# First norm rearranged with tables loaded later on; experts' output biases and the list of further rounds made behind the tenth expert

## The chip, the cores and the metric

One Trainium2 chip; the program runs on one of its cores. The metric is the device time of one execution in microseconds (us), as the median of several runs.

## What is computed

A decoder layer on 256 tokens of width 1024, all in float32: a norm whose scale and shift come from a condition vector, a mixer (softmax attention and gated linear attention side by side), a second norm and a mixture of 32 experts of which each token uses four, a final norm. Cut to what the change touches:

```
c_act = jax.nn.silu(c)
mod = (c_act @ w_ada[l] + b_ada[l])[:, None, :]
shift1, scale1, gate1, shift2, scale2, gate2 = jnp.split(mod, 6, axis=-1)
h = _rmsnorm(x, norm1_w[l]) * (1.0 + scale1) + shift1
x = x + gate1 * _mixer(h, w_in[l], gla_gate_w[l], gla_gate_b[l], gla_norm_w[l], w_o_moba[l], w_o_gla[l], b_merge[l], w_out[l])   # h @ w_in first, 1024 x 9232
h = _rmsnorm(x, norm2_w[l]) * (1.0 + scale2) + shift2
x = x + gate2 * _moe(h, w_router[l], b_router[l], w_exp_in[l], b_exp_in[l], w_exp_out[l], b_exp_out[l])
return _rmsnorm(x, final_norm_w)

# inside _moe, for the rows of expert e
hid = tokens[rows] @ w_exp_in[e] + b_exp_in[e]   # 1024 -> 2048
out = _clamped_swiglu(hid) @ w_exp_out[e] + b_exp_out[e]
out = out * wts[:, None]
```

One expert's weights are 8 MB (in) and 4 MB (out); the 32 of them are 403 MB of the 480 MB that the kernel moves.

## The kernel before

**Start.** The four quarters of x come transposed (`x0[u]`, 128 features by two by 256 tokens). Their squares are taken, two quarters on VectorE and two on ScalarE (`sx`). TensorE sums them over the features with 16 small products against a column of ones (into `pn_`), ScalarE takes the root (`rs1`), VectorE the reciprocal, TensorE spreads it over the partitions, ScalarE copies that to `rst`, and `scaled_x` multiplies x by it. Scale and shift of the norm are rows `cact @ w_ada`: `ada_rows(j)` makes those of features 256j to 256j+255 with eight products, from two blocks of `w_ada` of 1 MB each (`la[j][0]`, `la[j][1]`), and copies them out; `norm_unit` turns the rows into columns (`turn_rows`), adds the bias (`modT`, `s1`) and makes the normed features `hf`, their rounded half `hh` and the rest `hl`.

**First product.** It runs over j (four pairs of 128 features) and n (six blocks of 256 columns of w_in): `quarter` is 12 matmuls. Each weight block is split first into a rounded half `wh` (a copy on ScalarE, `split_hi`) and the rest `wl` (a subtraction on VectorE, `split_lo`); `splits(PAHEAD)` runs four blocks ahead. The weights come through a ring of 80 KB per partition (`ring`) in an order that is written out (`la`, `lw`); the first 80 KB are asked for at once, all on SyncE's queue (SP), later ones as blocks are used up (`Load.used`). The small weights `wgl` (16 columns of w_in) and `gw` come on ScalarE's queue.

**Mixer.** Everything up to the experts is written in an order that a planner makes as the program is built; the change does not move anything between the first product and the end of the mixer, except that the biases `b_exp_in` (`braw`) are asked for there.

**Experts.** The loop over e makes the hidden layer of expert e (`hidden`: 64 matmuls over four weight tiles), then the output of expert e - 1 (`output`: 32 matmuls over two tiles). For every second expert the rows of the next pair are gathered, and the finished pair is added into the four output banks `y` (`scatter`, called from within the next hidden layer through `later` and `between`). A tile is 2 MB; nine tiles fit, in rotation, so SP asks for a tile as soon as the tile nine places before it has been used up by TensorE:

```
rings = [ring] * 4 + [phase["r"]] * (RING2 // WE) + [ring]
def next_ring():
    rings.append(rings.pop(0))
    return rings[-1]
```

Around this loop stand two pieces of work that belong to no expert. `accumulators`, after the first hidden layer, turns the weights of the tokens (`wT`), spreads the second gate (`g2`) and multiplies the output biases `bo` by it; the function that it returns, called after the output of expert 0, adds the biases to `y` with four matmuls. `further_rounds`, after the output of expert 1, lists the experts that have more tokens than one round takes; the list is read only after the loop.

## Time and profile before

| | |
|---|---|
| median of 3 runs | 1297.88 us (1296.58 to 1302.86) |
| profiled execution, its own time | 1301.64 us |
| its span, first to last instruction | 1299.8 us |
| TensorE busy | 1227.0 us, 94% |
| VectorE, ScalarE, GpSimd busy | 422.1 us (32%), 294.2 us (23%), 7.6 us (1%) |
| moved | 480.13 MB, mean 369 GB/s |

A busy TensorE is not TensorE at its peak: matmuls are pipelined, and a slower clock shows as busy time too. The share of busy time is a mean over stages; what a change is worth in a stage is read from that stage. The first product starts at 22.6 us, the experts at 372.5 us. In the timeline "x8" counts what one line did in a stretch, and a float32 matmul counts as two.

### The profile page before, as it was taken

The page shows a single profiled execution, that of the slowest core. Times are in us where ns is not written, and L with a number is a line of the kernel's source. Part 1 is how long each engine was busy: PE and PEld are TensorE (multiplying, and loading weights), DVE is VectorE, ACT ScalarE, POOL GpSimd, SP SyncE. Part 2 cuts the span into 40 slices and gives each one's busy share as a digit, 9 for nine tenths or more (in the row PEclk, how much of TensorE's full clock was granted, in tenths as well). Part 3 has the DMA queues.
Part 4 walks back from the last instruction along what each step waited for, and adds up shares of the span by engine and source line. Part 5 has one row for each costly group of instructions (what it writes and reads, how often), then busy time and mean ns, then how long its engine had stood idle before and what let it go on. Part 6 is the DMA issues. An engine that isn't in the chain of part 4 may idle for free. (4 is left out here: it accounts for less than half of the span.)

```text
span 1299.8 us, 16460 instructions
## 1 busy us (share of the span) xinstructions
PE 1227.0 (94%) x6844; PEld 667.0 (51%) x6844; DVE 422.1 (32%) x849; ACT 294.2 (23%) x614; POOL 7.6 (1%) x13
## 2 busy tenths in 40 slices
PE   7999999999999899999999989898989989898995
PEld 5899989989854343443434424243433324242432
DVE  2567588866532211121112211111112212111112
ACT  2466567654321010110101101010101101010102
POOL 0000000000010000000000000000000000000000
PEclk9999999999899899999999999999999999999999
DMA  8997589584979999999999999999999999999994
GB/s 267 336 328 222 203 165 225 197 323 163 347 292 426 375 397 430 429 431 430 430 431 430 428 431 430 430 430 430 431 430 432 428 429 431 430 430 430 431 430 189
DMA packets 73436, 480.13 MB, mean 369 GB/s; under 512 B 7472, under 2 KB 24000, under 8 KB 48784
## 3 DMA queue, kind: packets, MB, share of 16 engines
q1 hardware_dynamic: 69664, 476.07, 92.0%
q10 hardware_dynamic: 3552, 2.69, 0.6%
q8 instruction: 55, 0.90, 0.3%
q0 software_dynamic: 144, 0.30, 0.1%
q14 instruction: 21, 0.17, 0.0%
HBM read 477.99 MB, written 1.05 MB: 369 GB/s over the span
## 5 line engine op out<-in xcount | busy, mean ns | idle before, releaser
L1306 PE MATMUL h<-w,xg 128*64 128x512 f32 x2048 | 464.4, 600 | 15.6 <-DMA w<-in_w_exp_in_dram 15.5
L1306 PEld LDWEIGHTS h<-w,xg 128*64 128x64 f32 x2048 | 140.6, 137 | 298.4 <-issue 269.4
L1340 PE MATMUL g<-w,aT 128*64 128x512 f32 x1024 | 232.3, 603 | 28.0 <-DMA w<-in_w_exp_out_dram 24.0
L1319 DVE TENSOR_SCALAR sg<-h 128x512 f32<-128x512 f32 x32 | 22.1, 692 | 520.0 <-PE h L1306 510.0
L400 PE MATMUL ps_a<-m,wh 128*128 128x256 f32 x896 | 172.0, 293 | 3.7 <-ACT m L510 3.7
L1340 PEld LDWEIGHTS g<-w,aT 128*64 128x64 f32 x1024 | 73.5, 138 | 172.9 <-issue 149.0
L400 PEld LDWEIGHTS ps_a<-m,wh 128*128 128x128 f32 x896 | 144.0, 197 | 6.8 <-ACT m L510 3.8
L1332 ACT COPY aT<-g 128x512 f32<-128x512 f32 x32 | 18.7, 586 | 506.2 <-PE g L1330 506.2
L400 PE MATMUL ps_a<-m,wl 128*128 128x256 f32 x448 | 129.1, 288 | 0.6 <-DVE wl L386 0.6
L386 DVE TENSOR_TENSOR wl<-w,wh 128x512 fp32r<-128x512 f32 x176 | 115.6, 685 | 38.7 <-ACT wh L382 37.3
L382 ACT CAST wh<-w 128x512 fp32r<-128x512 f32 x176 | 105.0, 617 | 67.2 <-PE ps_a L400 50.8
L1346 DVE TENSOR_TENSOR u<-g,u 64x512 f32<-64x512 f32 x64 | 44.1, 689 | 195.2 <-PE g L1340 194.5
L400 PEld LDWEIGHTS ps_a<-m,wl 128*128 128x128 f32 x448 | 88.2, 197 | 0.8 <-DVE wl L386 0.8
L1320 ACT ACTIVATE sg<-sg 128x512 f32<-128x512 f32 x32 | 20.2, 631 | 187.3 <-DVE sg L1319 187.3
L1239 PE MATMUL g<-Psel,u 128*128 128x128 f32 x512 | 60.4, 276 | 0.0
L1352 PE MATMUL y<-u,pT 128*128 128x512 f32 x128 | 59.2, 605 | 0.8 <-DVE u L1346 0.8
L1239 PEld LDWEIGHTS g<-Psel,u 128*128 128x128 f32 x512 | 58.5, 192 | 0.1
L1248 ACT ACTIVATE xg<-xg,shift 128x128 f32<-128x128 f32 x128 | 40.9, 390 | 27.7 <-DVE xg L1245 26.2
L1352 PEld LDWEIGHTS y<-u,pT 128*128 128x128 f32 x128 | 23.0, 189 | 36.8 <-issue 34.7
L400 PE MATMUL ps_a<-u,wh 128*128 128x256 f32 x224 | 40.7, 283 | 0.0
L400 PE MATMUL ps_a<-wh,m 128*128 128x256 f32 x192 | 34.9, 284 | 0.0
L400 PEld LDWEIGHTS ps_a<-u,wh 128*128 128x128 f32 x224 | 34.4, 189 | 0.0
(301 smaller groups left out, 887.0 us busy)
## 6 DMA issues: line engine op xcount, KB each, us to landing
w<-in_w_exp_in_dram SPq DMA_DIRECT2D x128, 2048.0 KB, 37.3
w<-in_w_exp_out_dram SPq DMA_DIRECT2D x63, 2048.0 KB, 37.7
w<-in_w_in_dram SPq DMA_DIRECT2D x26, 1024.0 KB, 14.3
w<-in_w_ada_dram SPq DMA_DIRECT2D x16, 1024.0 KB, 9.6
w<-in_w_ada_dram SPq DMA_DIRECT2D x32, 256.0 KB, 6.9
w<-in_w_in_dram SPq DMA_DIRECT2D x12, 512.0 KB, 8.0
w<-in_w_o_gla_dram SPq DMA_DIRECT2D x4, 1024.0 KB, 8.6
w<-in_w_o_moba_dram SPq DMA_DIRECT2D x4, 1024.0 KB, 7.1
```

Of the source, the lines that this page charges most:

```text
L382: S.copy(wh, wv)
L386: V.tensor_tensor(wl, wv, wh.bitcast(F32), op=OP.subtract)
L400: PE.matmul(o, lhsT, rhs, start=(b + k + n == 0), stop=(k == 7 and n == 2), skip_group_check=True)
L1239: PE.matmul(o, flat(hx[t, q])[:, 128 * kk:128 * kk + 128], P[:, t], start=(n == 0), stop=(n == 3))
L1248: S.activation(xg[:, kk, 0:w_], xg[:, kk, 0:w_], AF.Identity, bias=shift2[:, kk:kk + 1])
L1306: PE.matmul(ph[64 * hf_:64 * hf_ + 64, 512 * b:512 * b + 512], xg[:, k, SL * i:SL * i + SL], wi[k // 2][:, k % 2, 1024 * hf_ + 512 * b:102 ...
L1319: V.tensor_scalar(sg_, ph[:, 0::2], LIMIT, None, op0=OP.min)
L1320: S.activation(sg_, sg_, AF.Sigmoid, scale=ALPHA)
L1332: S.copy(aT, ps.rearrange("p (c s) -> p c s", c=4))
L1340: PE.matmul(po[64 * n:64 * n + 64, :], aT[:, cc, 64 * hf_:64 * hf_ + 64], wo[hf_][:, cc, 512 * n:512 * n + 512], start=(hf_ + cc == 0), st ...
L1346: V.tensor_mul(flat(og[n])[64 * par:64 * par + 64], po[64 * n:64 * n + 64], flat(g2[n])[64 * n:64 * n + 64])
L1352: PE.matmul(y[t, n], pT[0:rows, 128 * t:128 * t + 128], flat(og[n])[0:rows], start=False, stop=True, skip_group_check=True)
```

## The change

Six edits, in the order of the program.

1. `wgl` is laid out on the host, so that each partition reads one run of 512 bytes in place of eight of 64 bytes.
2. The blocks of `w_ada` come as two transfers in place of four, and the first blocks of `w_in` as one in place of two, with runs of 4 KB in place of 2 KB. Bytes, order and ring stay as they were.
3. The table for the root is asked for at once behind the sigmoid (`scrap`). VectorE adds the squares up, so that TensorE sums them with 2 products in place of 16. `ada_rows` is cut into halves: the first runs ahead of the sum of squares, the second behind the spreading of the reciprocal; the copy `rst` comes ahead of the copy of the rows.
4. `norm_unit(0)` comes ahead of `splits(PAHEAD)`.
5. `braw` is asked for on GpSimd's queue; `bo` is a tile of its own with one transfer.
6. `accumulators` is cut in two: `second_gate` stays, `add_biases` comes after the output of expert 12, its four matmuls within the hidden layer of expert 14; `further_rounds` comes after the output of expert 9.

```diff
-    return {"vec": np.ascontiguousarray(vec.T), "xf": np.ascontiguousarray(xf)}
+    thin = lambda w: np.ascontiguousarray(w.reshape(8, 128, -1).transpose(1, 0, 2).reshape(128, -1))
+    return {"vec": np.ascontiguousarray(vec.T), "xf": np.ascontiguousarray(xf),
+            "wgl": thin(np.asarray(inputs["w_in"])[0][:, C_GL:C_GL + 16])}
...
-                for k in range(0, 4, 2):
-                    for v in range(2):
-                        nc.sync.dma_start(wa[:, k:k + 2, v], kview(w_ada, D * v + 256 * j, D * v + 256 * j + 256,
-                                                                   4 * i + k, 4 * i + k + 2))
+                for v in range(2):
+                    nc.sync.dma_start(wa[:, :, v], kview(w_ada, D * v + 256 * j, D * v + 256 * j + 256,
+                                                         4 * i, 4 * i + 4))
...
-        def first_block(j, n0, n1):
+        def first_block(j, c0, c1):
             def emit():
-                wa = ring.tile([128, n1 - n0, 2, 512], F32, name="w")
-                for n in range(n0, n1):
-                    nc.sync.dma_start(wa[:, n - n0],
-                                      kview(w_in, C_GQ + 512 * n, C_GQ + 512 * n + 512, 2 * j, 2 * j + 2))
+                wa = ring.tile([128, 2, c1 - c0], F32, name="w")
+                nc.sync.dma_start(wa, kview(w_in, C_GQ + c0, C_GQ + c1, 2 * j, 2 * j + 2))
                 return wa
-            return queue(emit, 2 * (n1 - n0), 4 * KB * (n1 - n0))
+            return queue(emit, (c1 - c0) // 256, 8 * (c1 - c0))
...
+        scrap = mwork.tile([128, 1], F32, name="scrap")
         S.activation(cact, vec[:, R_C:R_C + 8], AF.Sigmoid)
+        S.activation(scrap, epst, AF.Sqrt)
         sx = [unit() for _ in range(4)]
-        for u in range(2):
-            V.tensor_mul(sx[2 * u], x0[2 * u], x0[2 * u])
-            S.activation(sx[2 * u + 1], x0[2 * u + 1], AF.Square)
-            if u == 0:
-                V.tensor_mul(cact, cact, vec[:, R_C:R_C + 8])
+        V.tensor_mul(sx[0], x0[0], x0[0])
+        S.activation(sx[1], x0[1], AF.Square)
+        V.tensor_mul(cact, cact, vec[:, R_C:R_C + 8])
+        V.tensor_mul(sx[2], x0[2], x0[2])
+        S.activation(sx[3], x0[3], AF.Square)
+        for u in (2, 1, 3):
+            V.tensor_tensor(sx[0], sx[0], sx[u], op=OP.add)
+        V.tensor_tensor(sx[0][:, 0], sx[0][:, 0], sx[0][:, 1], op=OP.add)
...
-        def ada_rows(j):
-
-            bk = Bank()
-            for i in range(2):
-                for k in range(4):
-                    PE.matmul(bk.t[32 * k:32 * k + 32, :], cact[:, 4 * i + k:4 * i + k + 1].to_broadcast([128, 32]),
-                              la[j][i].tv[:, k].rearrange("p v n -> p (v n)"), start=(i == 0), stop=(i == 1),
-                              skip_group_check=True)
-                la[j][i].used()
-            ev = unit()[:, :, 0:T].rearrange("p a b -> p (a b)")
+        def ada_rows(j, bk, i):
+
+            for k in range(4):
+                PE.matmul(bk.t[32 * k:32 * k + 32, :], cact[:, 4 * i + k:4 * i + k + 1].to_broadcast([128, 32]),
+                          la[j][i].tv[:, k].rearrange("p v n -> p (v n)"), start=(i == 0), stop=(i == 1),
+                          skip_group_check=True)
+            la[j][i].used()
+
+        def rows_out(bk):
+            ev = unit().rearrange("p a b -> p (a b)")
             S.copy(ev, bk.t)
             return bk, ev
-        pn_ = Bank()
-        for u in range(4):
-            for b in range(2):
-                for t in range(2):
-                    PE.matmul(pn_.t[:, t:t + 1], sx[u][:, b, 128 * t:128 * t + 128], ones[:, 0:1],
-                              start=(u + b + t == 0), stop=(u + b == 4), skip_group_check=True)
+        pn_, pr_ = Bank(), Bank()
+        ada_rows(0, pr_, 0)
+        for t in range(2):
+            PE.matmul(pn_.t[:, t:t + 1], sx[0][:, 0, 128 * t:128 * t + 128], ones[:, 0:1], start=True, stop=True)
         S.activation(rs1, pn_.t[:, 0:2], AF.Sqrt, bias=epst, scale=1.0 / D)
-        rows0 = ada_rows(0)
         V.reciprocal(rs1, rs1)
         for t in range(2):
             PE.matmul(pn_.t[:, 128 + 128 * t:256 + 128 * t], rs1[:, t:t + 1].to_broadcast([128, 128]), ident,
-                      start=True, stop=True, skip_group_check=True)
+                      start=True, stop=True)
+        ada_rows(0, pr_, 1)
         rst = unit()[:, 0]
         S.copy(rst, pn_.t[:, 128:384])
         pn_.free()
+        rows0 = rows_out(pr_)
...
-        S.dma_start(flat(wgl)[:, 0:128].rearrange("p (k n) -> p k n", k=8), kview(w_in, C_GL, C_GL + 16, 0, 8))
+        S.dma_start(flat(wgl)[:, 0:128], a["wgl"])
...
+        mod_unit(0, rows0)
+        norm_unit(0)
         splits(PAHEAD)
-        norm_unit(0, rows0)
...
-                    nc.sync.dma_start(flat(braw[n])[32 * i:32 * i + 32, :], a["b_exp_in"][0][:, c0:c0 + 512])
+                    G.dma_start(flat(braw[n])[32 * i:32 * i + 32, :], a["b_exp_in"][0][:, c0:c0 + 512])
...
-    bo = []
-    for n in range(2):
-        bo.append(flat(unit())[0:NE])
-        G.dma_start(bo[n], a["b_exp_out"][0][:, 512 * n:512 * n + 512])
+    bo_ = moe.tile([NE, 2, 512], F32, name="bo")
+    G.dma_start(bo_.rearrange("e n c -> e (n c)"), a["b_exp_out"][0])
+    bo = [bo_[:, n] for n in range(2)]
...
-    def accumulators():
-
-        wT = ew.tile([NE, T], F32, name="wT", bufs=1)
-        tp = psg.tile([128, 512], F32, name="g")
-        for t in range(2):
-            PE.transpose(tp[0:NE, 128 * t:128 * t + 128], wts[:, t], ident)
-        V.tensor_copy(wT, tp[0:NE, 0:T])
+    def second_gate():
+
         for n in range(2):
             ps = psg.tile([128, 512], F32, name="g")
             spread(ps, modT[:, 5, 4 * n:4 * n + 4])
             g2.append(unit())
             S.copy(flat(g2[n]), ps)
+
+    def add_biases():
+
+        wT = ew.tile([NE, T], F32, name="wT", bufs=1)
+        tp = psg.tile([128, 512], F32, name="g")
+        for t in range(2):
+            PE.transpose(tp[0:NE, 128 * t:128 * t + 128], wts[:, t], ident)
+        S.copy(wT, tp[0:NE, 0:T])
+        for n in range(2):
             V.tensor_mul(bo[n], bo[n], flat(g2[n])[0:NE])
...
-            add_biases = accumulators()
+            second_gate()
...
-        if e == 1:
-            add_biases()
-        if e == 2:
+        if e == 10:
             further_rounds()
+        if e == 13:
+            later.append(add_biases())
```

On TensorE the program begins so before: sums of squares (`ps_b<-ones,u`), rows (`y<-w,cact`), spreading (`ps_b<-kt,rs`), turning the rows (`y<-rows,u`), then the first product (`ps_a<-m,wh`).

```order
L365 MATMUL ps_b<-ones,u 128x1 x16
L353 MATMUL y<-w,cact 32x512 x8
L371 MATMUL ps_b<-kt,rs_182 128x128 x2
L345 MATMUL y<-rows,u 128x1 x4
L400 MATMUL ps_a<-m,wh 128x256 x2
```

And so in the change:

```order
L355 MATMUL y<-w,cact 32x512 x4
L368 MATMUL ps_b<-ones,u 128x1 x2
L372 MATMUL ps_b<-kt,rs_173 128x128 x2
L355 MATMUL y<-w,cact 32x512 x4
L349 MATMUL y<-rows,u 128x1 x4
L403 MATMUL ps_a<-m,wh 128x256 x2
```

Fourteen small matmuls are gone, and half of the rows stand ahead of the sum.

On ScalarE, at the same place, before: the root (`rs<-ps_b`), the copies of the rows and of `rst`, the two small transfers, four copies `wh`, then `hh` (`m<-u,modT,s`).

```order
L367 ACT_TABLE_LOAD
L367 ACTIVATE rs_182<-ps_b,epst 128x2
L358 COPY u<-y 128x512
L374 COPY u<-ps_b 128x256
L583 DMA u<-in_w_in_dram 128x8x16
L584 DMA u<-in_gla_gate_w_dram 16x512
L382 CAST wh<-w 128x512 x4
L510 ACTIVATE m<-u,modT,s_181 128x256 x2
```

In the change:

```order
L332 ACT_TABLE_LOAD
L332 ACTIVATE scrap<-epst 128x1
L335 ACTIVATE u<-u 128x512
L338 ACTIVATE u<-u 128x512
L369 ACTIVATE rs_173<-ps_b,epst 128x2
L376 COPY u<-ps_b 128x256
L362 COPY u<-y 128x512
L588 DMA u<-in_wgl_dram 128x128
L589 DMA u<-in_gla_gate_w_dram 16x512
L515 ACTIVATE m<-u,modT,s_172 128x256 x2
L385 CAST wh<-w 128x512 x6
```

The copies `wh` have moved behind `hh`, and VectorE's `wl` behind `hl` in the same way.

On TensorE behind the output of expert 0 (`g<-w,aT`), before: the way back of the next pair, the biases (`y<-u,wT`), the hidden layer of expert 2 (`h<-`), the output of expert 1 and the list (`g<-msk,ones`, `g<-kt,itc`).

```order
L1340 MATMUL g<-w,aT 64x512 x16
L1258 MATMUL g<-kt,pw 128x128 x2
L1215 MATMUL y<-u,wT 128x512 x4
L1298 MATMUL h<-bx,sel 128x512 x2
L1306 MATMUL h<-w,xg 64x512 x20
L1330 MATMUL g<-kt,li 128x128 x4
L1306 MATMUL h<-w,xg 64x512 x12
L1340 MATMUL g<-w,aT 64x512 x16
L1365 MATMUL g<-msk,ones 128x32 x2
L1376 MATMUL g<-kt,itc 1x128 x2
L1298 MATMUL h<-bx,sel 128x512 x2
```

In the change the same stretch reads:

```order
L1351 MATMUL g<-w,aT 64x512 x16
L1269 MATMUL g<-kt,pw 128x128 x2
L1309 MATMUL h<-bx,sel 128x512 x2
L1317 MATMUL h<-w,xg 64x512 x20
L1341 MATMUL g<-kt,li 128x128 x4
L1317 MATMUL h<-w,xg 64x512 x12
L1351 MATMUL g<-w,aT 64x512 x16
L1309 MATMUL h<-bx,sel 128x512 x2
```

The four matmuls of the biases and the four of the list are gone from it; they stand behind the output of expert 9 (the list) and in the hidden layer of expert 14 (the biases).

## Rows read from the trace of the kernel before

**Rows 1.** What TensorE waited for from 0 to 372 us, longest first: us in total, times, longest.

```profile
PE ps_b L365 <- DVE u L334: 5.7, 1, 5.7
PE ps_a L400 <- ACT m L510: 3.7, 1, 3.7
PE ps_a L1145 <- DVE msk L1142: 1.3, 1, 1.3
```

**Rows 2.** Timeline of the start, 0 to 36 us: start, duration (both us), engine, line, operation, output and inputs, shapes, count, and in brackets the idle time before and what ended it. DVE is VectorE, ACT is ScalarE.

```profile
5.69 6.99 PE L365 MATMUL ps_b<-ones,u 128*128 128x1 f32 x32 [5.69 <-DVE u L334]
...
7.87 0.63 ACT L335 ACTIVATE u<-u 128x512 f32<-128x512 f32 x1 [0.93 <-DMA u<-in_xf_dram]
...
8.52 1.28 ACT L367 ACT_TABLE_LOAD   x1
...
12.61 3.64 PE L353 MATMUL y<-w,cact 128*32 128x512 f32 x16
12.71 0.26 ACT L367 ACTIVATE rs<-ps_b,epst 128x2 f32<-128x2 f32 x1 [2.92 <-PE ps_b L365]
13.01 0.17 DVE L369 RECIPROCAL rs<-rs 128x2 f32<-128x2 f32 x1 [6.20 <-ACT rs L367]
...
16.18 1.22 PE L371 MATMUL ps_b<-kt,rs 128*128 128x128 f32 x4
16.31 0.58 ACT L358 COPY u<-y 128x512 f32<-128x512 f32 x1 [3.33 <-PE y L353]
...
17.19 1.71 PE L345 MATMUL y<-rows,u 128*128 128x1 f32 x8
...
17.84 0.69 DVE L580 TENSOR_TENSOR u<-u 128x512 f32<-128x512 f32 x1 [4.67 <-ACT u L374]
...
18.50 2.18 ACT L382 CAST wh<-w 128x512 fp32r<-128x512 f32 x4 [0.69 <-DMA w<-in_w_ada_dram]
...
21.56 0.15 DVE L498 TENSOR_TENSOR modT<-y,vec 128x4 f32<-128x4 f32 x1
...
21.95 1.09 ACT L510 ACTIVATE m<-u,modT,s 128x256 fp32r<-128x256 f32 x2 [1.27 <-DVE s L501]
...
22.60 1.05 PE L400 MATMUL ps_a<-m,wh 128*128 128x256 f32 x2 [3.71 <-ACT m L510]
```

**Rows 3.** Transfers of w_ada by the time at which SP issued them, KB each, median us from issue to landing: first the one issued from 3.1 us on (the fourth, last of block 0), then the one issued at 7.86 us (the eighth, last of block 1).

```profile
w<-in_w_ada_dram SPq DMA_DIRECT2D x1, 256.0 KB, 6.4
...
w<-in_w_ada_dram SPq DMA_DIRECT2D x1, 256.0 KB, 4.6
```

**Rows 4.** What SP's queue waited for from 0 to 40 us (`u<-in_w_in_dram` is the transfer of `wgl`, issued at 17.44 us), and the stretch from 20 to 22 us (stretch, its length, busy time of each engine with instructions, granted TensorE clock, share of the DMA engines, GB/s).

```profile
SPq L268 <- DMA u<-in_w_in_dram: 4.2, 1, 4.2
...
20.00:22.00 2.00, 0.00 (x0) 0.00 (x0) 1.93 (x6) 0.73 (x3) 0.00 (x0) 1.00 0.24 37
```

**Rows 5.** Timeline of the first product on TensorE, early and late in it; the third matmul of each three has a row of its own between these.

```profile
24.31 0.63 PE L400 MATMUL ps_a<-m,wh 128*128 128x256 f32 x2
...
24.95 0.63 PE L400 MATMUL ps_a<-m,wh 128*128 128x256 f32 x2
...
28.75 0.40 PE L400 MATMUL ps_a<-m,wh 128*128 128x256 f32 x2
...
29.11 0.40 PE L400 MATMUL ps_a<-m,wh 128*128 128x256 f32 x2
```

**Rows 6.** Stretches of the experts: stretch, its length, busy time and instructions of PE, PEld (weight loads), DVE, ACT and POOL, granted TensorE clock, share of the DMA engines, GB/s.

```profile
420.00:440.00 20.00, 20.00 (x74) 6.66 (x74) 0.00 (x0) 0.59 (x1) 0.57 (x1) 0.83 0.84 342
...
460.00:480.00 20.00, 20.00 (x108) 9.40 (x108) 4.49 (x10) 3.93 (x11) 0.00 (x0) 1.00 0.97 382
480.00:500.00 20.00, 20.00 (x96) 6.99 (x94) 2.07 (x4) 0.96 (x2) 0.00 (x0) 1.00 1.00 421
...
500.00:520.00 20.00, 20.00 (x84) 6.78 (x80) 4.34 (x9) 0.63 (x1) 0.00 (x0) 1.00 1.01 431
...
700.00:720.00 20.00, 18.34 (x84) 5.95 (x80) 3.84 (x6) 1.22 (x2) 0.00 (x0) 1.00 1.01 429
```

**Rows 7.** Timeline of TensorE in the first experts (columns as in rows 2): the hidden layer of expert 1, the biases, the hidden layer of expert 2, the first matmuls of the list, the hidden layer of expert 3.

```profile
392.24 8.80 PE L1306 MATMUL h<-w,xg 128*64 128x512 f32 x40
...
418.51 4.55 PE L1215 MATMUL y<-u,wT 32*128 32x512 f32 x8
...
424.15 10.72 PE L1306 MATMUL h<-w,xg 128*64 128x512 f32 x40
...
447.64 0.63 PE L1365 MATMUL g<-msk,ones 128*128 128x32 f32 x4
...
453.21 4.70 PE L1306 MATMUL h<-w,xg 128*64 128x512 f32 x16
```

**Rows 8.** Timeline of SP's queue: start, and the time from the first issue to the end of the last in the row. L138 issues the tiles of w_exp_in, L996 `braw`. The rows with x4 are the tiles of experts 3, 6 and 12.

```profile
324.48 9.99 SPq L996 DMA_DIRECT2D u<-in_b_exp_in_dram  x8
...
407.07 23.02 SPq L138 DMA_DIRECT2D w<-in_w_exp_in_dram  x4
...
499.59 11.44 SPq L138 DMA_DIRECT2D w<-in_w_exp_in_dram  x4
...
657.87 11.45 SPq L138 DMA_DIRECT2D w<-in_w_exp_in_dram  x4
```

**Rows 9.** Timeline of GpSimd from 360 us on: the first work on the biases `braw`.

```profile
369.86 0.61 POOL L1185 CAST bx<-u 128x512 fp32r<-128x512 f32 x1 [3.50 <-DVE wts L1161]
```

18 lines of the change are left out of this document (11 added, 7 removed).

## The prediction

> **What bounds the kernel now.** Three views were read in this order: the list of what TensorE waited for, the timeline of the start, and the stretches of the experts.
>
> Up to the experts TensorE sets the time. In the first 372 us it waits 5.7 us for the first squares, 3.7 us for `hh` ahead of the first product, and then never longer than 1.3 us at once [rows 1]. What the start gains, the whole mixer gains, as long as the weights keep up.
>
> In the experts the transfers set it. From 500 us on they run at 431 GB/s with the DMA engines full; TensorE is busy all of 500 to 520 us, but only 18.34 of the 20 us from 700 us on [rows 6], so by then it waits for weights. A tile of 2 MB takes 2.097 / 431 = 4.87 us, an expert (six tiles) 29.2 us. TensorE's own pace shows in SP's queue, which asks for a tile when TensorE has freed its place: from expert 6's tiles (499.59 us) to expert 12's (657.87 us) it took 158.3 us, 26.4 us for each [rows 8]. TensorE starts the experts behind the transfers, with all nine places full, and catches up 2.8 us per expert. While it is behind, a delay of TensorE frees a place late and the DMA engines idle; that time is never returned, since from then on they are full to the end. Such holes can be read: 342 GB/s from 420 to 440 us, 382 from 460 to 480 us, 421 from 480 to 500 us [rows 6].
>
> **The start, step by step.** Before, the sums of squares keep TensorE until 5.69 + 6.99 = 12.68 us, since 32 weight loads and matmuls take 0.218 us each; the rows follow at 12.61 us, the spreading at 16.18 us, and the first product at 22.60 us, 0.65 us behind the first `hh` [rows 2]. Between lies a detour: `modT` stands on VectorE behind four `wl` and comes only at 21.56 us, though the turned rows were there at 17.19 + 1.71 = 18.90 us [rows 2]. In the change:
>
> - The last square is ready at 7.87 + 0.63 = 8.50 us. ScalarE loads the root's table ahead of the squares: 1.28 us, which fits into its waits for x. One more addition on VectorE (0.69 us, as the 128x512 operation of line 580) and one of half the size (estimate 0.4 us) [rows 2] give the sum at 9.6 us.
> - Block 0 of `w_ada` landed at 3.1 + 6.4 = 9.5 us, block 1 at 7.86 + 4.6 = 12.5 us [rows 3]. The order and the bytes are the same, so I keep both. The first half of the rows, half of 3.64 us [rows 2], runs from 9.6 to 11.4 us.
> - Sum of squares, 4 x 0.218 us: 12.3 us. Root and reciprocal, from TensorE's end at 12.68 to 13.18 us before, 0.5 us: 12.8 us. Spreading 1.22 us: 14.0 us. Second half of the rows 1.82 us: 15.9 us. Copy 0.58 us: 16.5 us. Turning the rows, from the copy's end (16.89 us) to 18.90 us before, 2.0 us: 18.5 us. `modT` and `s1`, 21.56 to 21.95 us before, 0.4 us: `hh` starts at 18.9 us. [rows 2]
> - Now ScalarE makes both `hh` (1.09 us) before the first `wh` (2.18 / 4 = 0.55 us): the first product can start at 20.6 us, and its third matmul waits for `wl`, which VectorE ends about 0.7 us after `wh`; TensorE reaches it 0.4 us after its start (two matmuls at 0.64 us per three [rows 5]), so 0.3 us more. I count 21.0 us against 22.60 us. That is the term **-1.6 us**; bounds +1.3 and -4.3 us (rivals 1 and 2).
>
> The weights keep up. SP waited 4.2 us for the transfer of `wgl`, with its 1024 runs of 64 bytes, and could issue nothing; from 20 to 22 us the DMA engines moved 37 GB/s [rows 4]. With runs of 512 bytes I expect that hole gone. It is worth nothing in itself, because TensorE did not wait for a weight then [rows 1], but it covers the earlier start: the stream moves forward by more than TensorE does. Without that cover the 1.6 us would run into SP's hole. Larger transfers of the same bytes I count as nothing for the same reason. The copies `rst` and of the rows, and the halves of rows 1 to 3, do the same work in the same place.
>
> **The experts, step by step.** Taken off TensorE behind expert 0's output are the four matmuls of the biases, 4.55 us; the hidden layer behind them took 10.72 us for 40 against 8.80 us for the same 40 in expert 1 [rows 7], 1.9 us more, at a granted clock of 0.83 over that stretch [rows 6], a mixture of the levels 1.2 and 2.4 GHz. So about 6.5 us. Behind expert 1's output the list goes: from 447.64 us to the next hidden layer at 453.21 us [rows 7], 5.6 us less some 0.7 us of bias matmuls that stay, 4.9 us. These delays are longer than the holes that they leave, and I price the holes, because only they reach the end. SP's queue shows the first: four tiles of expert 3 took 23.02 us to issue [rows 8] where four take 11.45 us later, as the last place came free only in the delayed hidden layer of expert 2. The missing time of the DMA engines is (431 - 342) / 431 x 20 = 4.1 us, (431 - 382) / 431 x 20 = 2.3 us and (431 - 421) / 431 x 20 = 0.5 us [rows 6], **-6.9 us**. Both delays came before the end of these holes and nothing else in that stretch belongs to no expert. The bounds are 0 (the holes have another cause) and -7.1 us (also the 0.3 us or less that the turned weights of the tokens, now gone from behind expert 0, may have cost).
>
> What is moved comes back at experts 10 and 14: the same 4.9 and 6.5 us. TensorE has then caught up 2.8 us in each of some seven experts since 490 us, about 20 us, so four places are free and the DMA engines go on; that is the cover. Were it gone, up to 6.9 us would be lost again. VectorE's ten small operations and its product on `bo` come with these. The list's own transfer, 0.1 MB, ran ahead of a hole before and now stands in the full stream: 0.1 / 431, **+0.2 us**.
>
> The biases `braw` go from SP's to GpSimd's queue, eight issues. GpSimd's first work on them began at 369.86 us and waited for the end of the routing, not for them [rows 9]; SP had asked for them from 324.48 to 334.47 us [rows 8]. More than 30 us cover it. SP's tiles behind them come up to 10 us earlier, into places that wait for TensorE anyway: nothing.
>
> **Sum.** -1.6 - 6.9 + 0.2 = -8.3 us. The profiled execution took 1301.64 us (its span 1299.8 us and 1.8 us around it), so its like would take 1293.3 us. It lies 3.8 us above the median of the runs, 1297.88 us; from that, **1289.6 us**.
>
> **Rivals.**
>
> 1. *The first half of the rows delays the sum.* It stands ahead of the sum of squares and waits for block 0 of `w_ada`. If that lands only when block 1 did (12.5 us), everything behind moves from 9.6 to 12.5 us, and the product starts at 23.4 to 23.9 us: +0.8 to +1.3 us. For it: transfers of twice the size land later, each. Against it: the bytes ahead of block 0 are the same [rows 3]. Time 1297.88 + 1 - 6.7 = 1292.2 us.
> 2. *The clock rises earlier.* The first product ran at 0.64 us per three matmuls until past 24.95 us and at 0.36 us from 28.75 us on [rows 5]; of the two levels these are 1.2 and 2.4 GHz. The pitch tells it; the granted clock, 1.00 from 20 to 22 us [rows 4], does not. If the product met the higher level at its start, up to 28.75 - 22.60 = 6.1 us would shrink to 3.4 us: another -2.7 us, 1286.9 us. For it: the empty 3.7 us ahead of the product [rows 1] shrink to about 2. Against it: 13 us of TensorE work without a gap, from 5.69 to 18.90 us, left the clock low [rows 2]. The Trainium skill (TensorE: Matmul & The Clock Gate, Part 1, on the clock gate) says that the low clock is the resting state and sustained work releases it; by that rule alone the early part should have released it before, which this trace does not show.
> 3. *The holes stay.* TensorE is late at the start of the experts for another reason, say the lower clock of 420 to 440 us comes without the biases, and half of the 6.9 us remains: 1297.88 - 1.6 - 3.5 + 0.2 = 1293.0 us. For it: the clock fell in this stretch for no reason that a row names. Against it: the fall starts with the biases, and nothing like it stands in 500 to 520 us [rows 6].
> 4. *Slower: the clock stays low through the first product.* Its place is TensorE's short bursts from 9.6 to 18.5 us, with gaps that the trace of before does not have. Each quarter of 12 matmuls costs 4 x (0.64 - 0.36) = 1.1 us more at the low level [rows 5]; eight quarters more cancel the gain, 14 make the kernel slower by 0.5%, all 20 or so that ran at the higher one give 1289.6 + 22 = 1312 us. For it: a busy TensorE alone did not raise the clock before 22.6 us. Against it: the product itself did, within 6.1 us, and it is unchanged.
>
> **How the numbers follow.** A measurement of this kernel can tell about 0.5%, 6.5 us, from no change. My forecast has 0.56: 1287.5 to 1291.5 us. Rival 1 has 0.16, rival 2 has 0.11, rival 3 has 0.12, rival 4 has 0.05. Faster by over 0.5% (below 1291.4 us) are nearly all of the forecast and of rival 2, and a little of rivals 1 and 3: 0.69. Within 0.5% lie the rest of rivals 1 and 3: 0.26. Slower: 0.05. The range 1285.5 to 1294.5 us takes in rivals 1 to 3 and leaves out rival 4 and the ends of the unknown costs.
>
> **What would show it.** Right: the first product near 21.0 us, SP without a wait for `wgl`, and 300 GB/s or more from 20 to 22 us; 430 GB/s in every stretch from 380 us on (shifted by the start), the four tiles of expert 3 issued within 16 us, no hole near experts 10 and 14. TensorE would wait for weights from later than 700 us on, since the moved work takes up its lead. Wrong: a product that starts after 22.6 us; a hole that stays between 400 and 500 us; new holes at 640 to 760 us; or a mixer that is longer, from the first product to the experts, than the 349.9 us of before.

## The result, and the profile after

The change takes 1291.88 us (median of 9 runs, 1290.6 to 1295.24) against 1297.4 us for the kernel before (9 runs, 1295.47 to 1302.86): a ratio of 0.9946, interval 0.993 to 0.9962. That is 0.54% faster by the ratio (0.43% by the two medians), inside the range and 2.3 us above the number given. The runs of both kernels fall into two groups (of before six of nine at 1295.5 to 1297.9 us, three at 1301.2 to 1302.9; of the change six at 1290.6 to 1292.1, three at 1294.0 to 1295.2), the profiled execution of before, 1301.64 us, is of its upper group, that of the change, 1291.88 us, of its lower, and two single runs among those below, 4325 us (e3) and 2493 us (e10), are in no ratio.

**Start.** What TensorE waited for until the experts:

```profile
PE y L355 <- DMA w<-in_w_ada_dram: 10.6, 1, 10.6
PE ps_a L403 <- ACT wh L385: 2.1, 1, 2.1
```

What SP's queue waited for from 0 to 40 us (its longest wait), and the stretch that stood at 37 GB/s before [rows 4]:

```profile
SPq L269 <- DMA u<-in_wgl_dram: 5.7, 1, 5.7
```

```profile
20.00:22.00 2.00, 0.11 (x1) 0.11 (x1) 1.79 (x7) 1.76 (x4) 0.00 (x0) 1.00 1.06 405
```

SP still waits for `wgl`, longer than before, but the DMA engines stay full meanwhile. The timeline of the same stretch (columns as in rows 2; lines 355 to 403 answer to 353 to 400 of before):

```profile
9.83 0.42 DVE L341 TENSOR_TENSOR u<-u 128x256 f32<-128x256 f32 x1
...
10.65 1.93 PE L355 MATMUL y<-w,cact 128*32 128x512 f32 x8 [10.65 <-DMA w<-in_w_ada_dram]
12.51 1.01 PE L368 MATMUL ps_b<-ones,u 128*128 128x1 f32 x4
...
17.87 1.87 PE L349 MATMUL y<-rows,u 128*128 128x1 f32 x8 [0.70 <-ACT u L362]
...
21.89 0.80 PE L403 MATMUL ps_a<-m,wh 128*128 128x256 f32 x2 [2.15 <-ACT wh L385]
...
25.43 0.40 PE L403 MATMUL ps_a<-m,wh 128*128 128x256 f32 x2
```

The sum of the squares stands at 10.25 us (9.6 predicted), block 0 lets the rows start at 10.65 us (9.6), the product starts at 21.89 us (21.0 predicted, 22.60 before [rows 2]). Its two matmuls take 0.40 us, the higher level, from 25.43 us on, in before they did from 28.75 us [rows 5].

**Experts.** Stretches of the change (columns as in rows 6): three where the holes were, then those with the moved list and the moved biases. In the second fence the timeline of SP and TensorE there:

```profile
420.00:440.00 20.00, 20.00 (x92) 6.57 (x88) 4.75 (x9) 1.22 (x2) 0.00 (x0) 1.00 1.01 431
...
460.00:480.00 20.00, 20.00 (x96) 7.02 (x94) 2.01 (x5) 1.95 (x6) 0.00 (x0) 1.00 1.01 428
480.00:500.00 20.00, 20.00 (x84) 6.71 (x82) 4.74 (x9) 0.63 (x1) 0.00 (x0) 1.00 1.01 428
...
640.00:660.00 20.00, 14.06 (x54) 4.67 (x52) 7.15 (x19) 0.63 (x1) 0.00 (x0) 0.83 1.01 430
...
740.00:760.00 20.00, 19.54 (x68) 6.39 (x66) 2.86 (x5) 1.32 (x3) 0.00 (x0) 0.83 1.01 431
```

```profile
402.26 15.93 SPq L140 DMA_DIRECT2D w<-in_w_exp_in_dram  x4
...
646.77 3.65 PE L1351 MATMUL g<-w,aT 128*64 128x512 f32 x16 [1.09 <-DMA w<-in_w_exp_out_dram]
650.36 0.63 PE L1376 MATMUL g<-msk,ones 128*128 128x32 f32 x4
...
656.04 5.66 PE L1317 MATMUL h<-w,xg 128*64 128x512 f32 x16
...
745.75 4.14 PE L1226 MATMUL y<-bo,wT 32*128 32x512 f32 x8
```

342 and 382 GB/s [rows 6] have become 431 and 428. TensorE loses its time at the list (14.06 of 20 us busy) and the clock falls to 0.83 there and at the biases, as it did at 420 us before; the transfers run on at 430 and 431 GB/s.

**Where the time went.** The span splits where the first hidden layer starts: at 372.49 us before, at 369.28 us in the change. Behind that point 1299.8 - 372.49 = 927.3 us are left before, 1290.0 - 369.28 = 920.7 us after. So the experts give 6.6 us and all that is ahead of them 3.2 us, 9.8 us between these two executions. A mark behind the first product is the same group of small matmuls in the timelines, first of before, then of the change:

```profile
72.56 1.99 PE L551 MATMUL y<-u 16*128 16x256 f32 x8
```

```profile
70.69 1.99 PE L556 MATMUL y<-u 16*128 16x256 f32 x8
```

1.9 us of the 3.2 us are there by then. The other 1.3 us come from a fall of TensorE's clock late in the mixer, which lasted longer in this execution of before. The stretch from 330 to 340 us (columns as in rows 6; the clock is the third number from the end) in before, in the change, and in a second profile of the kernel before (e1), which has no fall there:

```profile
330.00:340.00 10.00, 10.00 (x61) 9.87 (x62) 4.54 (x11) 2.78 (x6) 0.00 (x0) 0.71 0.72 236
```

```profile
330.00:340.00 10.00, 10.00 (x71) 9.24 (x71) 5.27 (x11) 3.64 (x8) 0.00 (x0) 0.88 0.99 415
```

```profile
330.00:340.00 10.00, 10.00 (x80) 9.24 (x80) 6.03 (x13) 4.33 (x8) 0.00 (x0) 1.00 0.81 283
```

### The profile page after: what moved, and what is told of

It is laid out like the page before. It is cut to its first block, busy times and chain, and to the rows that moved or that the text cites. A ratio compares the mean times of both kernels' runs of the same rounds, so it can differ in the third digit from the quotient of the medians.

```text
span 1290.0 us, 16381 instructions
## 1 busy us (share of the span) xinstructions
PE 1216.9 (94%) x6816; PEld 657.5 (51%) x6816; DVE 423.5 (33%) x852; ACT 294.6 (23%) x616; POOL 11.2 (1%) x20
## 3 DMA queue, kind: packets, MB, share of 16 engines
HBM read 477.99 MB, written 1.05 MB: 371 GB/s over the span
## 5 line engine op out<-in xcount | busy, mean ns | idle before, releaser
L1351 PE MATMUL g<-w,aT 128*64 128x512 f32 x1024 | 228.7, 595 | 23.3 <-DMA w<-in_w_exp_out_dram 19.2
```

What stands on the lines that cost most here:

```text
L1351: PE.matmul(po[64 * n:64 * n + 64, :], aT[:, cc, 64 * hf_:64 * hf_ + 64], wo[hf_][:, cc, 512 * n:512 * n + 512], start=(hf_ + cc == 0), st ...
```

## The experiments

Every kernel was run beside the kernel before on the same chip; ratios are to that. e1 to e4, e5 to e8 and e9 to e12 shared one chip each; between these groups ratios are compared, not times. For each profile the span was split in the same way, in us. "Ahead" is the start of the first hidden layer, "behind" the rest of the span. "Ahead" is the sum of three parts: the time of the mark behind the first product, the mixer from there to the gather of the first experts' rows (`g<-Psel`), and the gather.

| kernel | profiled run | mark | mixer | gather | ahead | behind |
|---|---|---|---|---|---|---|
| before | 1301.64 | 72.56 | 295.64 | 4.29 | 372.49 | 927.3 |
| e1, before again | 1302.48 | 71.27 | 292.83 | 7.64 | 371.74 | 929.0 |
| e8, before, kept busy | 1297.47 | 70.97 | 295.43 | 4.30 | 370.70 | 925.0 |
| e5, order of the start alone | 1301.23 | 70.31 | 292.84 | 7.77 | 370.92 | 928.5 |
| e3, start alone | 1296.92 | 71.09 | 292.81 | 4.30 | 368.20 | 926.9 |
| e2, experts alone | 1291.13 | 72.15 | 292.83 | 4.30 | 369.28 | 920.0 |
| e4, biases alone | 1290.77 | 71.90 | 292.81 | 4.30 | 369.01 | 920.0 |
| the change | 1291.88 | 70.69 | 294.29 | 4.30 | 369.28 | 920.7 |
| e11, the change again | 1297.4 | 71.44 | 294.25 | 7.82 | 373.51 | 922.1 |
| e6, without biases and list | 1292.68 | 70.47 | 294.31 | 4.29 | 369.07 | 921.4 |
| e7, the change, kept busy | 1290.81 | 68.38 | 295.44 | 4.30 | 368.12 | 920.8 |
| e9, small w_ada transfers | 1292.91 | 70.36 | 295.65 | 4.30 | 370.31 | 920.8 |
| e10, old `wgl` | 1295.04 | 70.48 | 292.81 | 7.66 | 370.95 | 922.2 |
| e12, e9 kept busy | 1288.58 | 67.82 | 293.91 | 4.29 | 366.02 | 920.8 |

Behind: the five kernels whose biases stay behind expert 0 have 925.0 to 929.0 us (mean 927.3), the nine others 920.0 to 922.2 us (mean 921.0): 6.3 us, whatever the start does.

Ahead: the five profiles with the start of before (before, e1, e8, e2, e4) reach the mark at 70.97 to 72.56 us (mean 71.8), the four with edits 1 to 4 and nothing added there (the change, e11, e6, e3) at 70.47 to 71.44 us (mean 70.9). So the new start is worth about 0.85 us at the mark. At the experts it cannot be seen any more: e2 and e4, with the start of before, get there at 369.28 and 369.01 us, the change at 369.28 and 373.51 us. Two falls of the clock cover it. The mixer takes 292.8 us in all six profiles with a granted clock of 1.00 from 320 to 340 us and no products added (e1 to e5, e10), 294.3 us in the change, e11 and e6, 295.6 us in before and e9 (that of e7, e8 and e12 holds nine added products). And the gather takes 3.3 to 3.5 us longer in four profiles (e1, e5, e10, e11) than in the ten others; its 32 longer matmuls take 3.93 us in the change and 7.07 us in e11:

```profile
365.41 3.93 PE L1250 MATMUL g<-Psel,u 128*128 128x128 f32 x32
```

```profile
366.51 7.07 PE L1250 MATMUL g<-Psel,u 128*128 128x128 f32 x32
```

**e1: the kernel before, unchanged.**

> The kernel before, unchanged, for a second profile of it. Theory A (the terms were read from a slow execution): the profiled execution of before, 1301.64 us, had dips of the granted clock and holes in the transfers that an execution near the median lacks; if this profile belongs to an execution of 1296 to 1298 us, the missing transfer time from 380 to 500 us is 3 to 5 us in place of 6.9 us, and the first product still starts at 22.6 us. Theory B (the holes belong to the program): they are 6 to 7 us here too, at the same places, whatever the time; the 2.8 us that the change gained less than forecast is then lost elsewhere. The times equal those of before, within 0.1%.

1301.98 us (12 runs), ratio 0.9996, interval 0.9977 to 1.0015. Its profile has the product at 22.05 us and the holes in the same places:

```profile
420.00:440.00 20.00, 20.00 (x71) 6.64 (x71) 0.57 (x2) 0.59 (x1) 0.57 (x1) 0.83 0.86 347
440.00:460.00 20.00, 16.48 (x68) 5.63 (x65) 7.15 (x19) 0.63 (x1) 0.00 (x0) 0.91 1.00 428
460.00:480.00 20.00, 20.00 (x106) 9.56 (x106) 4.49 (x10) 3.94 (x11) 0.00 (x0) 1.00 0.98 382
```

On this chip most runs of the kernel before were of its upper group, so that the median is 4.6 us above that of the runs beside the change.

**e2: the experts' edits alone (6, and of edit 5 `bo`).** `braw` stays on SP's queue.

```diff
 # before, with `bo` as one tile and `accumulators` cut in two as in the change, and
-            add_biases = accumulators()
+            second_gate()
-        if e == 1:
-            add_biases()
-        if e == 2:
+        if e == 10:
             further_rounds()
+        if e == 13:
+            later.append(add_biases())
```

> Before, with only the move of the biases and of the list (and the biases' own tile); the start is that of before. Theory A: 3 to 4.5 us less than before, no hole from 380 to 500 us. Theory B: 6 to 7 us less, and the start then gives nothing or costs a little. The first product starts at 22.6 us in both.

1294.37 us (11 runs), ratio 0.9954, interval 0.9935 to 0.9972, 7.6 us below e1's median on the same chip; the ratio alone makes 6.0 us. So the experts' edits bring theory B's 6 to 7 us within the interval, and nearly all of what the whole change brings. 430, 430 and 428 GB/s at 420, 440 and 460 us.

**e3: the start alone (1 to 4).** The change with edits 5 and 6 undone.

> The change without the move of the biases and of the list, and with the biases of the experts' inputs on SP's queue again: only the start differs from before. Theory A: 1.5 to 2.5 us less than before, the first product at 21.9 us, the holes from 380 to 500 us as in before. Theory B: 0 to 1 us more than before, since the sum of both parts is 5.5 us and the experts alone give 6 to 7.

1298.34 us (12 runs), ratio 0.9982, interval 0.996 to 1.0005: that includes theory A's 1.5 to 2.5 us, and also no gain (1). The product starts at 21.62 us. Timeline of its biases and the hidden layer behind them, and its stretches:

```profile
414.20 3.69 PE L1223 MATMUL y<-u,wT 32*128 32x512 f32 x8
...
418.49 8.80 PE L1314 MATMUL h<-w,xg 128*64 128x512 f32 x40
```

```profile
420.00:440.00 20.00, 20.00 (x94) 6.64 (x90) 2.67 (x4) 1.22 (x2) 0.00 (x0) 1.00 0.99 410
440.00:460.00 20.00, 16.48 (x58) 5.71 (x56) 4.48 (x15) 0.00 (x0) 0.00 (x0) 0.83 0.98 401
460.00:480.00 20.00, 20.00 (x111) 9.60 (x111) 6.16 (x13) 4.30 (x12) 0.00 (x0) 1.00 0.95 373
```

Here the clock did not fall at the biases: they take 3.69 us and the 40 matmuls behind them 8.80 us, against 4.55 and 10.72 us [rows 7]. (It fell at the list, 0.83 from 440 to 460 us.) Holes remain, but smaller: by the working of the prediction, with 423, 429 and 429 GB/s in the three other stretches from 380 to 500 us, 5.6 us in place of the 7.3 us that the same six stretches of e1 give. e8, which has no fall at the biases either (3.70 and 8.80 us), gives 5.2 us. So by this working 5.2 to 5.6 us of the 7.3 us come from the work itself, and the rest goes with the fall of the clock.

**e4: the biases alone; the list stays behind expert 1.** Edit 6 without the move of `further_rounds`, and of edit 5 `bo` alone.

> Before, with only the biases moved to expert 14; the list stays behind the output of expert 1. If the biases make the hole from 420 to 440 us and the list the one from 460 to 490 us, each by itself, the first is gone and the second stays, and the gain is 4.1 of 6.9 parts of the gain of the run with both moved. If the list can use up the lead that TensorE has won without the biases, both holes are nearly gone and the gain is at least 0.9 of it. My own reckoning of the places, tile by tile, says the second.

1294.64 us (12 runs), ratio 0.9959, interval 0.9944 to 0.9974; "behind" is 920.0 us as in e2. TensorE still loses its time at the list, the transfers do not:

```profile
420.00:440.00 20.00, 16.48 (x81) 5.87 (x77) 6.31 (x15) 1.21 (x2) 0.00 (x0) 1.00 1.01 432
440.00:460.00 20.00, 20.00 (x77) 6.91 (x78) 0.85 (x4) 0.58 (x1) 0.00 (x0) 0.91 1.00 428
```

So without the biases ahead of it, TensorE is no longer so far behind that the list leaves a hole. The move of the biases is worth all of it, that of the list nothing on top; the list moved alone, with the biases behind expert 0, was not run, nor was `bo` as one tile without a move.

**e5: the order of the start alone (3 and 4), with the old transfers.** The change with edits 1, 2, 5 and 6 undone.

> Before, with only the order of the first norm changed (the table, the sums on VectorE, the rows in halves, the norm ahead of the splits); the transfers of w_ada, w_in and of the small weights are those of before, and so are the experts. Theory A (the order gives the gain of the start, the transfers only cover it): the first product starts at 21.6 to 21.9 us as in the run with the whole start, the gain is that run's, 1 to 2 us. Theory B (the transfers give it): the product starts at 22.6 us or later, or waits for weights within the first 40 us, and the time is that of before.

1298.32 us (12 runs), ratio 0.9986, interval 0.9966 to 1.0006. Its timeline:

```profile
8.68 3.15 PE L356 MATMUL y<-w,cact 128*32 128x512 f32 x8 [8.68 <-DMA w<-in_w_ada_dram]
...
11.76 0.61 PE L369 MATMUL ps_b<-ones,u 128*128 128x1 f32 x4
...
15.33 1.05 PE L350 MATMUL y<-rows,u 128*128 128x1 f32 x8 [0.70 <-ACT u L363]
...
18.54 0.80 PE L404 MATMUL ps_a<-m,wh 128*128 128x256 f32 x2 [2.15 <-ACT wh L386]
```

The product starts 3.35 us ahead of the change's. The sum of squares starts only 0.75 us earlier; the rest is the pitch of the same small matmuls behind it, which run at the higher level of the clock: the sum 0.61 us against 1.01, the spreading 0.71 against 1.23, the second half of the rows 1.06 against 1.94, the turning 1.05 against 1.87. Little of the lead lasts: at the mark it is 0.4 us (70.31 against 70.69 us), and the interval of the ratio includes 1, as e3's does.

**e6: the change without the output biases and with an empty list.** Both are left out of the computation.

```diff
         if e == 10:
-            further_rounds()
-        if e == 13:
-            later.append(add_biases())
+            zero = moe.tile([1, 2 * NIT], F32, name="zero")
+            V.memset(zero, 0.0)
+            V.tensor_copy(items, zero)
+            V.tensor_copy(nmore, zero[:, 0:1])
```

> The change, with the output biases left out and the list replaced by an empty one. Theory A (what was moved is hidden behind the transfers): the time is that of the change within 0.1%, and the transfers run at 430 GB/s from 380 to 1200 us in both. Theory B (the moved work still costs its 11 us of TensorE in part): 2 to 5 us less than the change.

1292.56 us (6 runs), ratio 0.9945, interval 0.9925 to 0.9966, the change's own ratio; 430 GB/s at 640 and 740 us. In its new place the moved work costs nothing that these runs can tell (their interval is 0.4% wide), and behind the start of the first hidden layer e6 has 921.4 us, the change 920.7 and 922.1 us.

**e7 and e8: TensorE kept busy.** e7 is the change with products of ones by ones ahead of the first rows (18), the first product (4), the base of the routing (4) and the routing (5); e8 is before with the last two alone.

```diff
+        def busy(o, n):
+            for _ in range(n):
+                PE.matmul(o, ones, ones, start=True, stop=True, skip_group_check=True)
...
+        busy(pn_.t[:, 384:512], 18)
         ada_rows(0, pr_, 0)
```

> The change, with products of ones by ones (128 x 128, into parts of banks that nothing else uses) where TensorE stands idle or does small work: 18 ahead of the first half of the rows, 4 ahead of the first product, 4 behind the first products of the router's bias, 5 ahead of the positions of the tokens. Theory A (the granted clock falls where TensorE has little to do, in some executions and not in others, and that spreads the times): the first product runs at the high level from its start, 0.36 us per three matmuls; no fall of the clock between 320 and 380 us; the times lie closer together and the median is 1.5 to 3.5 us below that of the change. Theory B (the falls have another cause): the clock falls as before at these places, and the time is that of the change or up to 2 us more for the added work.

> Before, with the same products of ones by ones at the last two of these places only (router's bias, positions); the start is that of before. Theory A: the upper half of the times of before, 1301 to 1304 us, goes down by 3 us or more, since it holds the executions in which the clock fell between 320 and 380 us; the lower half, 1296 us, stays; the median falls by 3 to 6 us. The hole from 420 to 440 us stays with the biases. Theory B: the times are those of before, 1 us up or down.

e7: 1290.8 us (6 runs), ratio 0.9937, interval 0.9916 to 0.9958, not to be told from the change's. Two signs of theory A are missing: from 320 to 330 us the clock falls to 0.83 all the same, and the product starts at 19.61 us but at the lower level: after 2.45 us in which TensorE waits for block 0, the granted clock is 0.66, then 0.50. A line of its timeline and two stretches:

```profile
10.04 1.06 PE L359 MATMUL y<-w,cact 128*32 128x512 f32 x8 [2.45 <-DMA w<-in_w_ada_dram]
```

```profile
12.00:14.00 2.00, 1.81 (x12) 0.74 (x12) 0.68 (x2) 0.37 (x1) 0.00 (x0) 0.66 1.04 424
14.00:16.00 2.00, 1.30 (x10) 0.41 (x3) 0.15 (x1) 0.58 (x1) 0.00 (x0) 0.50 1.05 378
```

e8: 1299.16 us (12 runs), ratio 0.9996, interval 0.9981 to 1.0011, with a narrower spread (1297.47 to 1301.68, against 1295.48 to 1306.16 of before beside it). The highest runs are gone, but the lowest too: no gain, against theory A. The added products did not hold the clock at the first of the two places: 0.85 from 330 to 340 us. At the second, none of the three profiles with products there (e7, e8, e12) has the fall at the gather, against four of the eleven others; that is too few to tell.

**e9 to e12: the start's transfers.** e9 is the change with the four transfers per block of `w_ada` of before, e10 the change with the old `wgl`, e11 the change itself, e12 is e9 with the products of e7. Before on this chip: 1299.6 us (14 runs, 1295.39 to 1303.75).

> The change with the four 0.25 MB transfers per block of w_ada of before in place of two of 0.5 MB; the runs of w_in and the contiguous wgl stay. Theory A (the larger transfers of w_ada land block 0 later and so cost the start its gain): the first half of the rows no longer waits until 10.65 us but starts at about 8.7 to 9.5 us, and the first product is seen before 20 us, against 21.89 us in the change. Since the product ran at half pace for longer in the run with all transfers small, the lead is down to 0.4 to 0.8 us at 65 us, and the time is 0.5 to 1 us below that of the change repeated beside it, which these runs can hardly tell. Theory B (the transfers of w_in or of wgl land block 0 later): the half still waits until past 10 us, and the product stays near 21.9 us.

1290.92 us (6 runs), ratio 0.9933, interval 0.9907 to 0.9958. Its timeline (PEld is the load of a matmul's weights):

```profile
8.65 3.15 PE L356 MATMUL y<-w,cact 128*32 128x512 f32 x8 [8.65 <-DMA w<-in_w_ada_dram]
9.87 0.19 PEld L356 LDWEIGHTS y<-w,cact 128*32 128x32 f32 x4 [1.04 <-DMA w<-in_w_ada_dram]
11.72 0.93 PEld L369 LDWEIGHTS ps_b<-ones,u 128*128 128x128 f32 x4 [1.66 <-issue]
...
20.29 0.80 PE L404 MATMUL ps_a<-m,wh 128*128 128x256 f32 x2 [2.15 <-ACT wh L386]
```

The half of the rows starts 1.4 us earlier than e11's (10.03 us), as expected, but waits again for its second transfer, and the sum of squares starts only 0.17 us earlier (11.72 against 11.89 us). So the larger transfers do not explain e5's lead of 3 us. The five profiles with larger transfers and no added products start the sum of squares at 11.86 to 12.51 us, e9 and e5 at 11.72 and 11.76 us: the larger transfers cost 0.1 to 0.8 us there. The product comes 1.0 us earlier (20.29 against 21.27 us), of which 0.8 us is again the clock, in the turning of the rows. It misses the 20 us of the expectation, and the time is not below e11's.

> The change with the old wgl, 1024 runs of 64 bytes cut out of w_in, in place of the contiguous copy. Theory A (the wait that SP has for wgl is a wait for places in the queues and not for its short runs, and the hole at 20 to 22 us came from the short runs keeping the DMA engines): SP still waits 4 to 6 us there, the DMA engines fall below 100 GB/s for 2 us, and no weight comes late for it: the time is within 1 us of the change repeated beside it. Theory B (the hole is what an earlier start runs into, as the prediction put it): TensorE waits more than 1 us for a weight between 22 and 60 us, and the time is 1.5 us or more above the change.

1292.61 us (8 runs), ratio 0.994, interval 0.9918 to 0.9962, that of e11 within what can be told, though the median is 1.9 us higher. SP's longest wait and one stretch:

```profile
SPq L267 <- DMA u<-in_w_in_dram: 9.6, 1, 9.6
```

```profile
26.00:28.00 2.00, 2.00 (x17) 1.79 (x17) 0.24 (x1) 0.00 (x0) 0.00 (x0) 1.00 0.20 25
```

The hole is there, later than before and as deep (25 GB/s for 2 us, where e11 moves 379 GB/s from 26 to 30 us), and SP waits 9.6 us, longer than theory A has it; but TensorE waits for no weight from 22 to 60 us, so in this start the hole costs TensorE nothing. The trace does not lay the 1.9 us to it: e10's mark, 70.48 us, is earlier than e11's, and e10 has the fall at the gather. The short runs make this hole, since e11 differs in nothing else. They are not the only way to one: e9, with the contiguous `wgl` but the small transfers of `w_ada`, moves 122 GB/s from 18 to 20 us.

> The change itself, on the same chip as its three variants. The prediction's sum stands at -8.3 us against an execution of the upper group of before; from what was measured so far I expect a median of 1291 to 1294 us, 5.5 to 7.5 us below the median of before on this chip.

1290.67 us (7 runs, 1290.49 to 1297.4), ratio 0.9941, interval 0.9918 to 0.9964; the median is 0.3 us below the range expected, and 8.9 us below that of before on this chip. The profiled run is its slowest, 1297.4 us. Its stretches ahead of the experts:

```profile
360.00:370.00 10.00, 8.25 (x51) 7.54 (x49) 4.93 (x22) 3.51 (x7) 2.11 (x3) 0.79 0.32 97
370.00:380.00 10.00, 10.00 (x43) 5.51 (x44) 2.40 (x8) 3.84 (x9) 2.15 (x3) 0.70 0.53 177
380.00:400.00 20.00, 20.00 (x106) 8.68 (x104) 3.27 (x7) 2.06 (x4) 0.00 (x0) 1.00 0.98 415
```

The clock fell at the first gather. The experts start 4.23 us later than in the change's own profile; 0.7 us of this is there at the mark and still there when the gather starts, 3.5 us come in the gather. A small hole follows: 4.23 + 922.1 - 920.7 = 5.6 us is the whole difference of the two spans. This is one program, twice.

> The change with the small transfers of w_ada and with products of ones by ones on TensorE in the gaps of the start, ahead of the base and ahead of the routing. Theory A (what the small transfers win at the start is kept if TensorE is at its higher level early): first product before 18.5 us, the higher pitch by 22.5 us, time 1 to 2.5 us below the change beside it. Theory B (the weights of the first product are the limit once the product starts this early): TensorE waits more than 2 us in all for transfers between 18 and 60 us, and the time is that of the change within 1 us.

1289.93 us (6 runs, 1288.58 to 1291.19), ratio 0.9927, interval 0.9903 to 0.9951: the lowest time of all kernels tried, though its interval overlaps e11's and the 0.7 us between the medians are less than the 1 us that theory A asked for; its product before 18.5 us and its pitch are there. Three lines of its timeline and one of its stretches:

```profile
17.48 0.50 PE L409 MATMUL ps_a<-m,wh 128*128 128x256 f32 x2 [1.16 <-ACT wh L391]
...
18.43 0.40 PE L409 MATMUL ps_a<-m,wh 128*128 128x256 f32 x2
...
366.02 13.95 PE L1326 MATMUL h<-w,xg 128*64 128x512 f32 x64
```

```profile
360.00:370.00 10.00, 10.00 (x70) 7.19 (x72) 4.68 (x16) 4.46 (x12) 4.39 (x5) 1.00 0.70 237
```

The product starts 3.8 us earlier than e11's and at the higher level (a short fall follows at 30 to 33 us); at 71 us the lead is 3.6 us, and with no fall of the clock ahead of the experts it is 7.5 us where they start (366.02 against 373.51 us).

## Why the prediction came out right, and where it did not

**The experts: right in place and size.** The sum had -6.9 + 0.2 = -6.7 us; the two profiles give 927.3 - 920.7 = 6.6 us behind the start of the first hidden layer, and the table of fourteen profiles 6.3 us. By the times, e2 has 6.0 us of the change's 7 us (ratios 0.9954 and 0.9946), with intervals of some 2 us either way. All three holes are gone, expert 3's four tiles were issued in 15.93 us (16 predicted, 23.02 before [rows 8]), and no hole came at experts 10 and 14; e6 shows no other cost there. That the holes are what counts, and not the delays, is shown by e4: the list's delay behind expert 1 stayed, left no hole and cost nothing.

Two readings inside this term were off. I let both delays share the holes; by e4 moving the biases alone takes them away. And not all of the holes come from the work: of the 7.3 us in six stretches, 1.7 to 2.1 us (7.3 less e3's 5.6 and e8's 5.2) go with the fall of the clock at the biases, which happens in some executions and not in others.

**The start: about half the size, and not by the steps.** The term was -1.6 us at the product; it is -0.7 us in the change's own profile (e11: -1.3, e3: -1.0). The first step that failed is the landing of block 0, 10.65 us in place of 9.5 (10.0 to 10.4 us in e10, e11 and e3), with the sum 0.65 us later than worked out; all the steps behind it took what they were given, within 0.2 us each. That is a good third of rival 1. Behind the first product, at the matmuls that start at 72.56 us before, the change is at 70.69 us: -1.9 us, close to the -1.6 us of the sum, but by luck. Before's profile is the latest of five with that start and the term was read from it; over all nine profiles the lead at this mark is 0.85 us. By the times the gain of the start alone is not shown (e3 and e5: both intervals include 1).

**The mixer: not in the sum.** From the product to the experts it took 347.4 us in place of 349.9 us. 1.2 us of this is the earlier rise of the clock (1.9 - 0.7), 1.3 us the shorter fall of the clock at 330 us. Neither is shown to be the change's doing: with the start of before e8 is at the higher level by 25.93 us, and e1, the kernel before once more, has no fall at 330 us at all. e11, the program of the change, took 352.2 us, with the fall at the gather. With the 0.3 us more at the start these 1.3 us make 9.8 of 8.3 us, less 0.1 us in the experts.

**The step that failed: from the profile to the median.** The sum was made for an execution of before's upper group, with a fall of the clock at the biases in it, and then taken off a median of three that lay in the lower group. Lower runs against lower runs the change gave 1296.6 - 1291.1 = 5.5 us, upper against upper 1302.0 - 1294.8 = 7.2 us (means of the groups of the result), all runs 6.1 us. -8.3 us was thus too much for the median by some 2 us: 1289.6 predicted, 1291.88 measured. That the time still lies inside the range is owed to the experts' term, which is most of the sum. Where upper runs of before are half or more, the medians differ by more (e11: 8.9 us).

What makes the groups is shown in part. Of the nine profiles with the biases moved, the two of runs above 1294 us (e10, e11) have the fall of the clock at the gather, 3.3 to 3.5 us, and the seven others do not. Of the five with the biases behind expert 0, the three above 1301 us have a fall at the biases (the 40 matmuls behind them take 10.72 us in before, 11.21 in e1, 11.09 in e5) and another ahead of the experts; e3 and e8, near 1297 us, have none at the biases and the smallest remainders of the five (926.9 and 925.0 us). No profile of a lower run of the unchanged kernel was taken, and why the clock falls in one execution and not in the next stays open.

**The smaller claims.** SP without a wait for `wgl`: wrong, 5.7 us. 300 GB/s or more from 20 to 22 us: right, 405. The reason given, that the change's gain would else run into the hole: wrong by e10. The larger transfers cost the start 0.1 to 0.8 us where I had nothing. `braw` on GpSimd: no run moves it alone; behind, e2 and e4, where it stays on SP, have 920.0 us, the change 920.7 us. TensorE waiting for weights from later than 700 us on: wrong by one wait, 1.09 us at 646.77 us, ahead of the list, so TensorE had caught up sooner than I counted; the next ones come behind 800 us. At the list it stands idle for 5.9 of 20 us, at no price.

**The rivals.** Rival 3 fell: no hole stays. Rival 4 fell: the higher level came no later than before, by 25.43 us in the change and 27.99 us in e11, against 28.75 us. Rival 1 happened in part. Rival 2 is not shown: with the start of before the higher level came anywhere from 25.93 us (e8) to 28.75 us, with the new one from 25.20 us (e6) to 27.99 us. The time measured lies at rival 1's 1292.2 us and outside the 1287.5 to 1291.5 us of the forecast itself, but rival 1's reason explains 1.1 us of the 2.3 us at most (rows from 10.65 us on in place of 9.6). The Trainium skill (TensorE: Matmul & The Clock Gate, Part 1, on the clock gate) says that the number of matmuls that one kernel runs at the lower clock differs from run to run; the two profiles of the change agree, with the higher level from 25.43 us after a product at 21.89 us, and from 27.99 us after one at 21.27 us.

## What to carry over

Where transfers are the bound to the end, price a delay of the engine ahead of them by the hole that it leaves in the transfers, not by its length, and put work that belongs to no tile where the engine has already caught up. Split the span at the point where the bound changes and compare the parts over many profiles: that gave 6.3 us with a spread of 2 to 4 us, where the times of one program spread by 5 to 7 us, and it showed that the 3.2 us ahead of the experts, between the first two profiles, were mostly a matter of which executions these were. Before a sum made from one profile is taken off a median, look in which group of runs that profile lies.

## What the runs showed of the hardware

- TensorE's clock falls in some executions of one program and not in others, at the same places. At 360 to 380 us the change had 1.00 in one profile and 0.79 and 0.70 in another, behind the same wait of 1.3 us; the gather took 3.5 us longer. At 328 to 336 us it fell in one profile of before and not in the other, worth 2.8 us of the mixer.
- Products of ones in the gaps of the start brought the first product to the higher level from its start in e12 (17.48 us, 0.50 us for the first two matmuls, 0.40 us from 18.43 us on), but not in e7, where 2.45 us without work came ahead of the rows. The level shows in the small matmuls too: the eight that turn the rows took 1.05 us in e5, e9 and e12, 1.87 us in the change.
- One transfer of 0.5 MB in place of two of 0.25 MB let the first use start 1.4 us later (10.03 against 8.65 us), but the last use ended nearly at the same time, 0.17 us apart (e9 against e11).
- A queue that waits for a transfer is not the same as idle DMA engines: SP waited 5.7 us for `wgl` in the change, and the engines moved 392 to 406 GB/s from 18 to 24 us; it waited 4.2 us before, and they moved 37 GB/s from 20 to 22 us [rows 4].
